# Differential heads moved beside the projections and the sliding heads, and the out-projection done whole, by token chunk, with the norm beside it

## The chip, the cores and the metric

The kernel runs on one core of a Trainium2 chip. Its time is the device time of one execution, in microseconds (us); the time of a kernel is the median of several executions. TensorE (PE) does the matmuls, VectorE (DVE), ScalarE (ACT) and GpSimd (POOL) the rest, and SyncE (SP) issues most of the DMAs.

## The reference, cut to what matters

Two layers of a trunk over 128 context tokens and 1024 latent tokens, 1024 wide. Each layer normalises its input, projects it to queries, keys and values of three groups of heads, attends, projects the heads' outputs and adds them to the residual; then a gated feed-forward part with a convolution over three positions.

```python
x_n = rmsnorm(x, g) * (1 + scale) + shift           # scale, shift, gate: from a modulation matmul
qa, ka, va, qb, kb, vb, qc, kc, vc = split(x_n @ w_in)   # A: 4 heads, B: 8 heads over 2 kv, C: 4 heads
oa = neighborhood_attn(qa, ka, va, cache, rpb)      # A: 8 rows x 16 columns around the token
ob = window_attn(qb, kb, vb, cache, sink)           # B: |i - j| <= 128, in blocks of 128
o1 = dense_attn(qc[0], kc[0], vc); o2 = dense_attn(qc[1], kc[1], vc)   # C: all 1024 + 256 keys
oc = rmsnorm(o1 - lam * o2, subln_g) * (1 - lam_init)
x = x + gate * (concat(oa, ob, oc) @ w_out)
x = x + gate2 * (silu(conv(h @ w_up)[g]) * conv(h @ w_up)[v]) @ w_down   # h: the norm of x again
```

## The kernel before

All of it is float32. A matrix that is to be multiplied is split into a high and a low part of a faster float32 form, and `gemm` (L488) makes three matmuls of each pair of blocks: high with high, high with low, low with high. `wload` (L366) loads a 128x1024 block of weights on SP's queue into `wraw` (two buffers), ACT writes the high part into `whl` (two buffers), and POOL or DVE subtracts for the low part. Activations lie transposed, with 128 features on the partitions and the 1156 token columns (128 context, 1024 latent, four of padding) in three chunks of some 386. So one block of 128 output features and one chunk of tokens over all 1024 input features is 24 matmuls.

A layer has 18 column blocks in its input projection (`inproj`), 54 groups of 24 gemms. Blocks 0 to 5 belong to the neighbourhood heads (A), 6 to 11 to the sliding heads (B), 12 to 17 to the differential heads (C). The queries and keys that it makes are normalised, turned by the rotary tables, split and written to DRAM, from where the attention loads them through POOL's queue.

The order of the work is that of the code, within what a scheduler that estimates times makes of it when the kernel is built: each engine gets one fixed row of instructions. `PLAN` names the steps of the input projection and of the heads that run in it: `A:4+2` projects blocks 4 and 2 side by side, `fA` opens the pool of the neighbourhood heads, `a:0` is head 0 of them, `b:0` the four sliding heads of one key and value head. In the order of the code a head stands ahead of the projections that come after it, so that these fill what it leaves free.

Every attention block is 128 queries. Its scores go to PSUM, in one of three banks named `s`; DVE takes the negative row maximum while it copies them into `P`; ACT takes the exponential with the row sum; PE transposes `P` in pieces of 128 into one of two banks `tb`; ACT copies these to `pt`; PE multiplies them with the values into the one bank `pv`; ACT copies the result into `O` (`tpv`, L644). Banks are given out in the order of the code. A differential head (`attnC`, L687) works on pairs of blocks, 256 queries, and has two components for each: scores, maxima and exponentials are made twice over 1280 keys, the second exponential is scaled and added to the first on POOL (L743, L744), and then one transpose and one product with the values do for both. The tiles `P` (128x1280) have seven buffers, and a head's queries and keys have two.

After the last step of `PLAN`, the four differential heads run in a pool of their own. Beside them stand the modulation pieces 4 to 11 (layer 0 only, four loads of 512 KB each) and, in `outproj_part`, the out-projection of the outputs of A (features 0 and 1) and B (2 to 5), whose raw outputs come back from the DRAM tile `odr`. This adds to the residual `x` in SBUF after each part. When the differential heads are done, the last part (features 6 and 7) follows, chunk 0 first and then chunks 1 and 2 together; `stats` squares the new `x` and `norm_apply` makes the feed-forward part's input of it. The last group of the down-projection goes the same way: chunk 0, then 1 and 2, and the norms of 1 and 2 behind both.

The change touches the main loop in `run`, `PLAN`, buffer numbers, `newO`, `finO`, the merge in `attnC`, and the weights `woa`, `wob`, `woc`.

## Time and profile before

| | |
|---|---|
| median of three runs | 3512.76 us (3512.06 to 3513.54) |
| the profiled execution | 3506.57 us |
| its span, first to last instruction | 3504.8 us |
| busy: PE, DVE, ACT, POOL | 95%, 58%, 43%, 35% |
| mean granted clock of TensorE | 0.971 |

The span falls into stages that repeat in both layers. Layer 0's first neighbourhood score starts at 147 us, the first sliding one at 313, the first differential one at 536; PE leaves attention at 889, ends the out-projection at 925 and runs the feed-forward part's gemms without a gap from 978 us on. In layer 1 these are 1907, 2075, 2301, 2597, 2637 and 2725. The feed-forward parts, some 770 us each, fill the rest.

PE's busy share is high everywhere and says little, because matmuls are pipelined and a matmul that has started late still counts as busy. What a stage leaves free is seen in the busy times of the other engines, in the granted clock, and in the number of matmuls that a stretch gets done. A group of instructions has its busy time (overlaps counted once), the mean of one in ns, and the idle time ahead of it.

### The profile page before, as it was taken

The page shows a single profiled execution, that of the slowest core. Times are in us where ns is not written, and L with a number is a line of the kernel's source. Part 1 is how long each engine was busy: PE and PEld are TensorE (multiplying, and loading weights), DVE is VectorE, ACT ScalarE, POOL GpSimd, SP SyncE. Part 2 cuts the span into 40 slices and gives each one's busy share as a digit, 9 for nine tenths or more (in the row PEclk, how much of TensorE's full clock was granted, in tenths as well). Part 3 has the DMA queues.
Part 4 walks back from the last instruction along what each step waited for, and adds up shares of the span by engine and source line. Part 5 has one row for each costly group of instructions (what it writes and reads, how often), then busy time and mean ns, then how long its engine had stood idle before and what let it go on. Part 6 is the DMA issues. An engine that isn't in the chain of part 4 may idle for free. (4 is left out here: it accounts for less than half of the span.)

```text
span 3504.8 us, 54130 instructions
## 1 busy us (share of the span) xinstructions
PE 3322.5 (95%) x20398; PEld 3012.4 (86%) x20398; DVE 2043.1 (58%) x4666; ACT 1505.4 (43%) x2905; POOL 1213.5 (35%) x1252
## 2 busy tenths in 40 slices
PE   6999998897899999999999989989888999999999
PEld 4987885684699999999989878858667999999999
DVE  5355466665676765676573554567667544544445
ACT  4566575545432222222245656665564322232222
POOL 6444246645611111111154442476565111111110
PEclk9999998897899999999999999999989999999999
DMA  5764338413112222222136652363201011111112
GB/s 202 203 162 130 94 100 217 133 37 93 34 61 73 85 76 67 82 85 78 43 125 189 169 134 74 109 165 82 52 17 36 32 46 44 43 37 46 46 40 93
DMA packets 184565, 318.21 MB, mean 91 GB/s; under 512 B 58544, under 2 KB 126528, under 8 KB 183920
## 3 DMA queue, kind: packets, MB, share of 16 engines
q1 hardware_dynamic: 170320, 266.18, 24.7%
q0 software_dynamic: 13984, 48.57, 6.8%
q8 instruction: 162, 2.65, 0.3%
q14 instruction: 99, 0.81, 0.1%
HBM read 260.15 MB, written 58.73 MB: 91 GB/s over the span
## 5 line engine op out<-in xcount | busy, mean ns | idle before, releaser
L496 PE MATMUL mm<-h,whl 128*128 128x386 f32 (+2 forms) x4488 | 888.0, 345 | 9.8 <-DVE h L484 4.3
L496 PEld LDWEIGHTS mm<-h,whl 128*128 128x128 f32 x4488 | 796.4, 190 | 29.3 <-DVE h L484 5.8
L496 PE MATMUL s<-h,whl 128*128 128x386 f32 (+2 forms) x4152 | 781.9, 342 | 15.7 <-ACT h L483 10.6
L496 PEld LDWEIGHTS s<-h,whl 128*128 128x128 f32 x4152 | 740.2, 190 | 29.9 <-ACT h L483 15.3
L378 POOL TENSOR_TENSOR whl<-wraw,whl 128x1024 fp32r<-128x1024 f32 x88 | 211.5, 2403 | 1344.5 <-ACT whl L377 1258.2
L685 ACT ACTIVATE P<-P,nm 128x641 f32<-128x641 f32 (+5 forms) x360 | 345.3, 960 | 169.5 <-DVE nm L734 89.6
L377 ACT ACTIVATE whl<-wraw 128x1024 fp32r<-128x1024 f32 (+1 forms) x210 | 207.5, 988 | 450.0 <-PE s L496 255.9
L496 PE MATMUL s<-ah,whl 128*128 128x384 f32 (+1 forms) x1268 | 356.6, 341 | 1.6 <-DVE x L918 1.2
L654 ACT ACTIVATE pt<-tb 128x512 f32<-128x512 f32 (+2 forms) x456 | 237.0, 541 | 147.2 <-PE tb L652 144.1
L652 PE MATMUL tb<-ident,P 128*128 128x128 f32 x1600 | 269.8, 289 | 14.9 <-ACT pt L654 7.5
L661 PE MATMUL pv<-pt,v 128*64 128x128 f32 x3200 | 264.0, 287 | 6.6 <-ACT pt L654 2.9
L918 DVE SCALAR_TENSOR_TENSOR x<-s,m,x 128x128 f32<-128x128 f32 (+3 forms) x347 | 170.0, 514 | 153.6 <-PE s L496 153.2
L918 DVE SCALAR_TENSOR_TENSOR x<-mm,m,x 128x128 f32<-128x128 f32 (+3 forms) x357 | 175.2, 513 | 142.1 <-PE mm L496 141.7
L652 PEld LDWEIGHTS tb<-ident,P 128*128 128x128 f32 x1600 | 189.7, 145 | 72.9 <-issue 36.3
L496 PE MATMUL mm<-ah,whl 128*128 128x384 f32 (+1 forms) x844 | 244.1, 340 | 1.4 <-DVE x L918 1.4
L661 PEld LDWEIGHTS pv<-pt,v 128*64 128x64 f32 x3200 | 173.7, 138 | 83.3 <-issue 54.6
L496 PEld LDWEIGHTS s<-ah,whl 128*128 128x128 f32 x1268 | 233.6, 189 | 5.9 <-DVE x L918 1.7
L496 PE MATMUL mm<-o,whl 128*128 128x384 f32 (+1 forms) x972 | 210.4, 354 | 11.7 <-ACT o L639 6.6
L496 PE MATMUL s<-al,whl 128*128 128x384 f32 (+1 forms) x634 | 215.1, 339 | 0.0
L496 PEld LDWEIGHTS mm<-o,whl 128*128 128x128 f32 x972 | 178.2, 197 | 24.5 <-issue 7.4
L682 PE MATMUL s<-k,q 128*128 128x256 f32 (+2 forms) x816 | 178.5, 333 | 19.2 <-DMA q<-d 11.5
L744 POOL TENSOR_TENSOR P<-P 128x1280 f32<-128x1280 f32 (+1 forms) x72 | 192.2, 2671 | 4.5
(208 smaller groups left out, 4971.8 us busy)
## 6 DMA issues: line engine op xcount, KB each, us to landing
wraw<-wup SPq DMA_DIRECT2D x88, 512.0 KB
mraw<-wmod SPq DMA_DIRECT2D x48, 512.0 KB
mraw<-wmv SPq DMA_DIRECT2D x96, 256.0 KB
wraw<-wdn SPq DMA_DIRECT2D x64, 384.0 KB
k<-d POOLq DMA_DIRECT2D x80, 288.5 KB, 6.5
wraw<-win SPq DMA_DIRECT2D x36, 512.0 KB
d<-hl SPq DMA_DIRECT2D x28, 386.0 KB
q<-d POOLq DMA_DIRECT2D x32, 289.0 KB, 6.6
```

The lines of the kernel that those rows point to most:

```text
L377: nc.scalar.activation(hl[:, 0, :n], raw[:, :n], AF.Copy)
L378: lo_eng.tensor_tensor(hl[:, 1, :n], raw[:, :n], hl[:, 0, :n].bitcast(F32), op=ALU.subtract)
L496: nc.tensor.matmul(ps, w_, r_[:, a:b], start=(i == 0), stop=(i == tot - 1))
L652: nc.tensor.transpose(t[:, 128 * j:128 * j + 128], it[0], self.ident)
L654: nc.scalar.activation(pt[:, :n], t[:, :n], AF.Copy)
L661: nc.tensor.matmul(ps[64 * i:64 * i + 64, :128], V[:, vb], pts[g // 4][:, 128 * (g % 4):128 * (g % 4) + 128], start=first[i], stop=left[i] ...
L682: nc.tensor.matmul(dst, q, view(ks[i]), start=(i == 0), stop=(i == 1))
L685: self.nc.scalar.activation(P[:, :n], P[:, :n], AF.Exp, scale=-1.0, bias=nm, accum_out=sums)
L744: nc.gpsimd.tensor_tensor(P2[0][:, :n], P2[0][:, :n], P2[1][:, :n], op=ALU.add)
L918: nc.vector.scalar_tensor_tensor(xx, ps[:, s - a:e - a], m[:, col + ob, v:v + 1], xx, op0=ALU.mult, op1=ALU.add)
```

## The change

- `PLAN` projects the C blocks beside the neighbourhood heads, then runs the differential heads 0 and 1 in front of the B blocks.
- After the projections, the differential heads 2 and 3 and all eight sliding heads run as two interleaved generators: after each step of a differential head (the context block, or a pair of blocks) four steps of the sliding heads (one block of queries each), and in layer 0 one modulation piece.
- The out-projection comes after all heads: for each token chunk, eight column blocks over all eight feature blocks, 24 gemms each, with the sums of squares behind each column block and the chunk's norm behind the eighth. Its weights are loaded once for each chunk, 24 loads of 512 KB a layer where there were 8; the low part is made by DVE and POOL in turn. The outputs of A and B are read back from `odr` in `loado`, and split as before.
- In `attnC` the merge of the two components goes to DVE for the first block of a pair and the context block, in one operation, and stays on POOL for the second.
- The last group of the down-projection goes chunk by chunk, each with its norm, and loads its weights three times and not twice.
- `P` of the differential heads has five buffers for seven, the projections' `t` six for seven; queries, keys and values of the sliding heads have more. Pools change sides from layer to layer.

```diff
-PLAN = "A:4+2 A:0 A:5+3 A:1 mF fA a:0 a:1 a:2 a:3 xA B:11 B:10+6 B:7+8 fB b:0 B:9 b:1 xB C:16 C:17 C:14+12 C:15+13"
+PLAN = "A:4+2 A:0 A:5+3 A:1 mF fA a:0 a:1 a:2 a:3 xA C:16 C:14+12 C:17 C:15+13 fC c:0 c:1 B:11 B:10+6 B:7+8 B:9"
-NQ_B, NK_B, NV_B, NP_B, NT_B = 3, 2, 1, 6, 5
-NQ_C, NK_C, NV_C, NP_C, NT_C = 2, 2, 1, 7, 4
+NQ_B, NK_B, NV_B, NP_B, NT_B = 4, 4, 2, 6, 6
+NQ_C, NK_C, NV_C, NP_C, NT_C = 2, 2, 1, 5, 4
...
-                cp, cs = self.open("C")
-                self.attnC(cp)
+                bp, bps = self.open("B")
+                gb = self.chain(self.attnB(bp, kv) for kv in range(2))
+                for n, _ in enumerate(self.chain(self.attnC(ap, h) for h in (2, 3))):
+                    for _ in range(4):
+                        next(gb, None)
+                    if todo and n > 0:
+                        self.mod_piece(l, todo.pop(0), md, self.mm(), NMC)
+                for _ in gb:
+                    pass
...
-                self.outproj_part(x, ab, 0, 2, a["woa"][l])
...
-                self.outproj_part(x, ab, 2, 4, a["wob"][l])
...
-                for ts in ((0,), (1, 2)):
+                for t in range(3):
+                    c0, c1 = OCHUNK[t]
                     for ob in range(KT):
-                        if ob % 4 == 0:
-                            whl = self.wload(a["woc"][l, ob // 4], nc.vector)
...
+                        whl = self.wload(a["wo"][l, ob], nc.gpsimd if ob % 2 else nc.vector)
+                        ps = self.mm()
+                        self.gemm(ps[:, :c1 - c0], whl, range(8), None, ow[t], 0, c1 - c0)
+                        self.addx(x, ob, ps, c0, c1, 16)
+                        self.stats(np_, x, stats[t], t, [ob])
+                    self.norm_apply(np_, hp0 if t == 0 else hp1, x, stats[t], t, "f")
...
-                for ts in ((0,), (1, 2)):
+                for t in range(3):
...
-                    self.down(x, *last, ts, after)
+                    self.down(x, *last, (t,), after)
...
+    def loado(self, pool, t):
...
+            nc.sync.dma_start(hl.bitcast(F32), self.odr[k, :, c0:c1])
+            nc.scalar.activation(hh, hl.bitcast(F32), AF.Copy)
+            nc.gpsimd.tensor_tensor(hl, hl.bitcast(F32), hh.bitcast(F32), op=ALU.subtract)
...
-                    nc.vector.scalar_tensor_tensor(ss[:, 1:2], ss[:, 1:2], lam[:, 1:2], ss[:, 0:1], op0=ALU.mult, op1=ALU.mult)
-                    nc.gpsimd.tensor_scalar(P2[1][:, :n], P2[1][:, :n], ss[:, 1:2], 0.0, op0=ALU.mult, op1=ALU.add)
-                    nc.gpsimd.tensor_tensor(P2[0][:, :n], P2[0][:, :n], P2[1][:, :n], op=ALU.add)
+                    nc.vector.tensor_scalar(ss[:, 1:2], ss[:, 1:2], ss[:, 0:1], lam[:, 1:2], op0=ALU.mult, op1=ALU.mult)
+                    if i == 0:
+                        nc.vector.scalar_tensor_tensor(P2[0][:, :n], P2[1][:, :n], ss[:, 1:2], P2[0][:, :n], op0=ALU.mult, op1=ALU.add)
+                    else:
+                        nc.gpsimd.tensor_scalar(P2[1][:, :n], P2[1][:, :n], ss[:, 1:2], 0.0, op0=ALU.mult, op1=ALU.add)
+                        nc.gpsimd.tensor_tensor(P2[0][:, :n], P2[0][:, :n], P2[1][:, :n], op=ALU.add)
```

How the change moves instructions is seen in the built programs' rows. In them `h` is a split chunk of the normalised input, `o` and `oc` are split outputs of the heads, `whl` weights, `mraw` modulation weights, `k`, `q`, `v`, `P` and `pt` the tiles of attention; `mm`, `s`, `tb` and `pv` are PSUM banks. Line numbers of the changed kernel differ a little: the same line stands four lower up to L728 (L496 is now L492), and L768 is L769.

The first place is PE in a differential head of layer 1. Before, its scores (L732) stand among small groups of output gemms:

```order
L661 MATMUL pv<-pt,v 64x128 x4
L673 MATMUL tb<-ident,sums 128x128 x4
L732 MATMUL s<-k,q 128x512
L496 MATMUL mm<-o,whl 128x386 x6
L661 MATMUL pv<-pt,v 64x128 x4
L652 MATMUL tb<-ident,P 128x128
L496 MATMUL mm<-o,whl 128x384
L732 MATMUL s<-k,q 128x512
L496 MATMUL mm<-o,whl 128x384 x3
L732 MATMUL s<-k,q 128x512
```

Now the scores of head 0 (L728) stand among groups of projection gemms:

```order
L728 MATMUL s<-k,q 128x512 x2
L728 MATMUL s<-k,q 128x256 x2
L492 MATMUL mm<-h,whl 128x386 x22
L728 MATMUL s<-k,q 128x512
L492 MATMUL mm<-h,whl 128x386
L728 MATMUL s<-k,q 128x512
L492 MATMUL mm<-h,whl 128x386
L728 MATMUL s<-k,q 128x512
L519 MATMUL mm<-t,ones_88 128x386
L583 MATMUL mm<-ident,qg 128x128 x3
L492 MATMUL mm<-h,whl 128x384 x21
```

The filler moved from the output gemms, which end in one DVE addition for each 6 or 12 of them, to the projection's, which end in a norm and a rotation for each 24. From head 0's first score to the first sliding score stand 456 of them in layer 1.

The second place is PE in layer 0 around the modulation pieces (L392, now L388). Before, they stand between the differential heads' scores:

```order
L732 MATMUL s<-k,q 128x256
L392 MATMUL mm<-mraw,cvz 32x512 x2
L732 MATMUL s<-k,q 128x256
L661 MATMUL pv<-pt,v 64x128 x4
L652 MATMUL tb<-ident,P 128x128
L732 MATMUL s<-k,q 128x512
L392 MATMUL mm<-mraw,cvz 32x512 x2
L732 MATMUL s<-k,q 128x512
L396 MATMUL mm<-sel,mrow 128x2 x4
```

Now this stands between the end of head 1 and the first sliding score (L678); two L388 matmuls use one load:

```order
L388 MATMUL mm<-mraw,cvz 32x512 x6
L769 MATMUL tb<-sq,ones_86 128x386
L648 MATMUL tb<-ident,P 128x128
L657 MATMUL pv<-pt,v 64x128
L388 MATMUL mm<-mraw,cvz 32x512 x2
L392 MATMUL mm<-sel,mrow 128x2 x4
L519 MATMUL mm<-t,ones_86 128x386
L388 MATMUL mm<-mraw,cvz 32x512 x8
L392 MATMUL mm<-sel,mrow 128x2 x4
L388 MATMUL mm<-mraw,cvz 32x512 x8
L392 MATMUL mm<-sel,mrow 128x2 x4
L388 MATMUL mm<-mraw,cvz 32x512 x6
```

So 30 of the 64 modulation matmuls, and with them 15 loads, stand ahead of the first sliding score, where before they were spread over the heads.

The third place is POOL in layer 0's norm for the feed-forward part, at chunk 1 of the out-projection. Now the low parts of weights (L374) stand between the steps of the norm (L475) and the sums of squares (L452):

```order
L374 TENSOR_TENSOR whl<-wraw,whl 128x1024
L452 TENSOR_TENSOR nsq<-nsq 128x386
L475 TENSOR_SCALAR nh<-nh,gf_8609,m_104 128x128
L475 TENSOR_SCALAR nh<-nh,gf_8609,m_104 128x256
L475 TENSOR_SCALAR nh<-nh,gf_8609,m_104 128x128
L475 TENSOR_SCALAR nh<-nh,gf_8609,m_104 128x256
L475 TENSOR_SCALAR nh<-nh,gf_8609,m_104 128x128
L475 TENSOR_SCALAR nh<-nh,gf_8609,m_104 128x256
L452 TENSOR_TENSOR nsq<-nsq 128x386
L475 TENSOR_SCALAR nh<-nh,gf_8609,m_104 128x128
L475 TENSOR_SCALAR nh<-nh,gf_8609,m_104 128x256
L374 TENSOR_TENSOR whl<-wraw,whl 128x1024
```

Before, POOL made no low part for the out-projection (DVE made all eight); the norm's steps ended with those of chunks 1 and 2 in one row, and the feed-forward part's weights followed:

```order
L479 TENSOR_SCALAR nh<-nh,gf_9293,m_107 128x128
L479 TENSOR_SCALAR nh<-nh,gf_9293,m_107 128x256
L444 TENSOR_TENSOR ny<-ny 128x386
L444 TENSOR_TENSOR ny<-ny 128x388
L479 TENSOR_SCALAR nh<-nh,gf_9293,m_107 128x386 x16
L378 TENSOR_TENSOR whl<-wraw,whl 128x1024 x42
```

What moved is that twelve low parts a layer now wait in POOL's row among the norm's steps.

## Rows read from the trace of the kernel before

**Rows 1.** Busy us of each engine (records), granted clock, DMA share, GB/s, by stage.

```profile
147.00:313.00 166.00, 158.15 (x1104) 136.53 (x1103) 85.39 (x239) 103.87 (x243) 74.84 (x102) 0.99 0.58 150
313.00:536.00 223.00, 218.61 (x1743) 191.01 (x1743) 123.20 (x393) 145.04 (x340) 87.72 (x162) 0.99 0.41 106
536.00:889.00 353.00, 303.79 (x1941) 214.90 (x1939) 210.73 (x628) 183.62 (x339) 200.68 (x163) 0.88 0.41 115
925.00:978.00 53.00, 43.64 (x201) 37.20 (x200) 45.72 (x67) 26.09 (x47) 38.63 (x34) 0.94 0.09 30
1907.00:2075.00 168.00, 156.25 (x1106) 135.57 (x1104) 86.62 (x241) 104.16 (x243) 76.05 (x105) 0.98 0.59 150
2075.00:2301.00 226.00, 223.01 (x1741) 192.33 (x1741) 124.77 (x395) 146.03 (x343) 88.29 (x168) 0.98 0.43 106
2301.00:2597.00 296.00, 256.46 (x1747) 200.09 (x1745) 200.98 (x611) 173.77 (x323) 193.15 (x151) 0.93 0.29 76
2637.00:2725.00 88.00, 78.35 (x382) 69.35 (x381) 70.32 (x118) 35.54 (x60) 41.02 (x36) 0.94 0.09 31
```

**Rows 2.** The same view, PE, PEld, DVE, ACT, POOL, for short stretches.

```profile
675.00:700.00 25.00, 18.52 (x96) 8.85 (x93) 9.88 (x33) 10.33 (x19) 17.97 (x22) 0.89 0.97 245
2215.00:2290.00 75.00, 75.00 (x593) 63.60 (x592) 47.48 (x143) 54.01 (x126) 36.93 (x68) 1.00 0.37 99
2310.00:2340.00 30.00, 26.84 (x202) 17.05 (x200) 24.70 (x91) 24.83 (x46) 23.08 (x15) 1.00 0.61 210
2365.00:2415.00 50.00, 49.04 (x345) 41.51 (x345) 40.22 (x126) 30.56 (x54) 34.64 (x25) 0.98 0.18 53
2526.00:2595.00 69.00, 54.71 (x367) 36.72 (x367) 42.71 (x133) 41.13 (x74) 44.91 (x25) 0.83 0.10 20
```

**Rows 3.** Timeline of PE in the feed-forward part: start, us, instructions.

```profile
2700.30 4.41 PE L496 MATMUL mm<-h,whl 128*128 128x386 f32 x24
2704.55 4.40 PE L496 MATMUL s<-h,whl 128*128 128x388 f32 x24
```

**Rows 4.** DVE groups: differential stage (two), sliding stage (two), L770 (ns min/median/max).

```profile
L734 DVE CUSTOM_DVE_ANT_0 P<-s,zero,nm 128x512 f32<-128x512 f32 (+1 forms) x128 | 76.0, 611 | 17.8 <-PE s L732 16.1
L740 DVE RECIPROCAL sums<-ss 128x1 f32<-128x1 f32 x32 | 5.1, 159 | 7.8 <-ACT P L685 7.6
...
L538 DVE TENSOR_TENSOR qg<-qg,rope 128x386 f32<-128x386 f32 (+1 forms) x15 | 10.6, 707 | 0.2
L443 DVE SCALAR_TENSOR_TENSOR t<-mm,t 128x386 f32<-128x386 f32 (+1 forms) x15 | 8.4, 557 | 11.2 <-ACT t L442 11.2
...
L770 DVE SCALAR_TENSOR_TENSOR O<-O,pp,oy x12: 604/682/3239, 692.3 to 2603.0; 128x386 f32<-128x386 f32 x8, 128x384 f32<-128x384 f32 x4
```

**Rows 5.** The larger of POOL's two merge operations, differential stage of layer 1.

```profile
L744 POOL TENSOR_TENSOR P<-P 128x1280 f32<-128x1280 f32 (+1 forms) x36 | 95.4, 2653 | 2.3
```

**Rows 6.** ACT groups: sliding stage of layer 1 (three), differential stage (two).

```profile
L685 ACT ACTIVATE P<-P,nm 128x641 f32<-128x641 f32 (+2 forms) x68 | 51.4, 758 | 33.6 <-DVE nm L821 16.4 <-issue 13.9 <-DVE nm L815 2.2
L665 ACT ACTIVATE O<-pv 128x128 f32<-128x128 f32 x32 | 8.8, 276 | 20.3 <-PE pv L661 20.2
L589 ACT ACTIVATE qg<-mm 128x384 f32<-128x384 f32 x6 | 2.9, 478 | 0.5 <-PE mm L587 0.4
...
L685 ACT ACTIVATE P<-P,nm 128x1280 f32<-128x1280 f32 (+3 forms) x76 | 93.1, 1226 | 38.2 <-DVE nm L734 37.7 <-DVE sums L740 0.4
L665 ACT ACTIVATE O<-pv 64x128 f32<-64x128 f32 (+1 forms) x40 | 10.8, 271 | 27.9 <-PE pv L661 27.4
```

**Rows 7.** POOL groups from 2597 to 2725, out-projection's end and norm of layer 1.

```profile
L479 POOL TENSOR_SCALAR nh<-nh,gf,m 128x386 f32<-128x386 f32 (+2 forms) x32 | 29.7, 938 | 4.6 <-ACT h L483 2.9 <-DVE nh L477 1.7
L456 POOL TENSOR_TENSOR nsq<-nsq 128x386 f32<-128x386 f32 (+1 forms) x12 | 15.1, 1269 | 5.5 <-ACT nsq L452 5.4
L378 POOL TENSOR_TENSOR whl<-wraw,whl 128x1024 fp32r<-128x1024 f32 x6 | 14.4, 2406 | 43.0 <-ACT whl L377 42.9
L640 POOL TENSOR_TENSOR o<-O,o 128x384 fp32r<-128x384 f32 (+1 forms) x6 | 5.6, 966 | 0.0
```

151 lines of the change are left out of this document (67 added, 84 removed).

## The prediction

> **What bounds the kernel now.** The first view is the table of busy time by stage, cut at the first scores of each kind of head [rows 1]. In both layers the stage of the neighbourhood heads (166 and 168 us) and that of the sliding heads (223 and 226 us) have projection gemms between their own matmuls, and PE is busy for 93% or more. The stage of the differential heads is the loose one: 353 us in layer 0 and 296 us in layer 1, with PE at 86 and 87%, DVE at 60 and 68%, ACT at 52 and 59%, POOL at 57 and 65%, and a granted clock of 0.88 and 0.93. No engine is full there. The short stretches say why [rows 2]: at 2310 to 2340, with no gemm beside, DVE and ACT reach 82 and 83% of the time; at 2365 to 2415, with output gemms beside, DVE reaches 80%; at 675 to 700, where layer 0 waits for modulation weights, DVE and ACT fall to 40% while the queues move 245 GB/s. Then come 36 and 40 us for the last part of the out-projection (889 to 925 and 2597 to 2637) and the norm's tail: 201 PE records in 53 us, 382 in 88 us [rows 1]. A gemm takes 4.25 us for 24 when nothing stops it, 0.177 us [rows 3], so 53 - 201 x 0.177 = 17 us and 88 - 382 x 0.177 = 20 us are lost there. The region that the change rewrites is thus 166 + 223 + 353 + 36 + 17 = 795 us in layer 0 and 168 + 226 + 296 + 40 + 20 = 750 us in layer 1.
>
> **The change, part by part.** *Stage 1, the neighbourhood heads*, keeps its order and about its number of gemms; the fill comes from the C columns now. I leave it at 166 and 168 us.
>
> *Stage 2, heads 0 and 1 beside the B columns.* It holds two differential heads and 456 gemms, and DVE is the first limit. Seven DVE rows of the four heads, from 76.0 us to 5.1 us, sum to 174, so 87 for two [rows 4]. The projections cost DVE 3.0 us a q or k chunk (five rows, from 0.707 us down to 0.557), and 16 chunks make 48. New on DVE is the merge of the second component for every other block, one operation over 128x1280 with two SBUF inputs, eight in the stage. No row has it. The nearest is L770 over 386 columns: 0.604 us at best, 0.682 in the median, 3.239 at worst [rows 4]. Scaled by columns the best is 2.0 us; the worst adds the same delay once, 4.6 us. I take 2.3, by the median, and have 18 us. The sum is 153 us of durations. Durations overlap: in the old sliding stage twelve ACT rows, from 51.4 us to 2.9, sum to 169 us [rows 6] where ACT was busy for 146 [rows 1], a factor of 0.87. That gives 133 us busy; at 80% it is 166 us, at the old stage's 68% it is 196. I take 195, the upper end, because six weight splits are not in the sum and because 72 of the 456 gemms are still to come when the second head's scores end, and the sliding heads' keys can be loaded only behind the last of them. POOL gives up half of its merges, whose larger half alone took 95.4 us for four heads [rows 5]; it was no limit, so that is worth nothing by itself.
>
> *Stage 3, heads 2 and 3 with all sliding heads.* No gemm is left as filler but layer 0's modulation pieces, and ACT is the first limit. Four ACT rows of the sliding heads, from 51.4 us to 8.8, sum to 116 us for 32 of 36 query blocks, so 130; four of the differential heads, from 93.1 us to 10.8, sum to 169, half is 84 [rows 6]. These 214 us of durations are 186 us busy. At the 83% of the best stretch that is 225 us, at the 72% of 2215 to 2290 [rows 2] it is 258, at the old differential stage's 59% it is 317. I take 255: two streams without gemms in PE's queue should do a little better than 72%, but the first loads and the last head's tail are in it too. PE is not the limit: in layer 1's old sliding stage 223 us of PE less 456 x 0.177 leave 142 us for 1285 attention records, 0.111 us each at most, and 2103 records (36/32 of these and half of the differential stage's 1315) make 233 us at most. In layer 0 fifteen modulation loads stand ahead of the first sliding score in PE's order, as its rows above show: 7.9 MB at 245 GB/s [rows 2] are 32 us, of which the loads of keys would take some 10 anyway. So layer 0 gets 275 us; before, its pieces lay in three places and cost 353 - 296 = 57.
>
> *Stage 4, the out-projection.* 576 gemms at 0.177 us are 102 us. Most of them ran beside heads before; now they stand alone, and beside them run the norm, 24 splits of outputs and 24 weight loads in place of 8. POOL has 29.7 + 15.1 us of norm, 12 weight splits at 2.406 us and 24 output splits at 0.966 us [rows 7]: 97 us, nearly as much as PE. PE runs 24 gemms, 4.25 us, between one weight and the next, and POOL's order, shown above, has eight norm operations and a sum of squares between two weights. I give 12 us for weights that come late, 8 for the entry from attention, 3 for sums of squares and 3 for the exit (the last norm has 96 gemms, 17 us, of other chunks to hide behind): 128 us. Bounds: 113 if POOL is never late, 150 if each of 12 weights waits for three norm operations of 0.938 us [rows 7]. This replaces the 36 + 17 and 40 + 20 us, and it is where the gain goes that stages 2 and 3 make.
>
> *The last down-projection* by chunk has 12 weight loads for 8 and a norm beside it; DVE was 80% busy in a norm's tail already (70.32 of 88 us [rows 1]), so I give it 4 us of gain, between 0 and 8. Pools, sides and smaller buffers are priced at nothing: five P buffers for seven make a pair's second block wait for the first one's merge, which the other stream covers in stages 2 and 3; uncovered, the wait is an exponential (1.226 us [rows 6]) and the merge, 3.5 us a pair and 28 us for the eight pairs of a stage.
>
> **The sum.** Layer 0: 166 + 195 + 275 + 128 = 764, 31 less. Layer 1: 168 + 195 + 255 + 128 = 746, 4 less. With 4 for the passage between layers it is 39 us. The profiled execution took 3506.6 us around its span of 3504.8, so 3468; the median of the runs is 6.2 us above it, hence **3474 us**.
>
> **A rule against it.** L770 shows what a DVE operation on SBUF may take: 3.239 us where 0.604 do [rows 4]; POOL's merges beside it take 2.653 us each [rows 5]. The Trainium skill (SBUF — State Buffer, "SBUF: two separate sides") says that a DVE operation with two SBUF inputs and a GpSimd operation hold one port pair by an exclusive lock, and that the loser waits for the whole instruction. By that, each merge on DVE could cost 2.3 us more than I gave it; in stage 2, where DVE sets the pace, sixteen in both layers make 37 us, and the total would be 3511 us; the trace agrees in the worst case, not in the median.
>
> **Rivals.** (a) *The two streams fill each other*: ACT at 83% and DVE at 80%, stages of 225 and 166 us, 59 less a layer, **3356 us**. For it: the stretch without a gemm. Against it: that lasted 30 us. Chance 0.20. (b) *The two streams wait for each other's banks*, the slower side: three banks for scores, two for transposes and one for PV are given out in program order, so a late sliding block holds up a differential one behind it. With ACT at 63% stage 3 takes 295 us, 40 more a layer, **3554 us**. It decides from about 275 us on, where the total equals that of before. For it: with seven P buffers, heads alone had ACT at 60% at 2526 to 2595 [rows 2]. Chance 0.20. (c) *POOL holds up the weights*: stage 4 at 150 us, **3518 us**. For it: 97 us of POOL beside 105 of PE; against it: the old norm's tail lost only 20. Chance 0.13. (d) *The clock falls without gemms*, as to 0.83 at 2526 to 2595 [rows 2]: 233 us at that clock are 281, 26 more a layer, **3526 us**; against it the clock of 1.00 at 2310 to 2340 with no gemm either. Chance 0.05. The Trainium skill (TensorE: Matmul & The Clock Gate, "Part 4: PE-mode transpose") says that full clock does not engage for transposes; the trace does not agree where scores and PV stand between them. (e) The forecast, 3430 to 3505 us: 0.42.
>
> **Chances.** 0.2% is 7 us, about what a measurement of this kernel can tell from no change. Faster: (a), 0.40 of the forecast, 0.03 of (c): 0.63. Same: 0.02 of the forecast, 0.05 of (c): 0.07. Slower: (b), (d), 0.05 of (c): 0.30. The range leaves out half of (a) and half of (b): 3360 to 3555 us.
>
> **What would show it.** Cut the new profile at the first score of each kind of head: stage 2 at 166 to 196 us with DVE at 68 to 80%; stage 3 at 225 to 295 us with ACT first, longer in layer 0 with a low clock at its start; stage 4 at 113 to 150 us with POOL about as busy as PE. The forecast is wrong if ACT in stage 3 is outside 65 to 80%, if the DVE merge has a mean outside 2.0 to 4.6 us, or if weights and not gemms set stage 4.

## The result, and the profile after

The changed kernel takes 3649.75 us (3647.89 to 3650.73) where the kernel before takes 3512.41 in the same session: a ratio of 1.0392, 95% interval 1.0374 to 1.0410. That is 137 us slower, where 39 us faster were forecast. In the experiments below the kernel before ran in each session; its medians lie between 3506 and 3512 us, so ratios are compared, and 0.1% is 3.5 us.

The page of the changed kernel begins so (busy us, then the clock in tenths over 40 slices of 91 us):

```profile
span 3648.0 us, 54000 instructions
PE 3370.6 (92%) x20398; PEld 3042.0 (83%) x20398; DVE 2070.1 (57%) x4590; ACT 1537.8 (42%) x2941; POOL 1148.6 (31%) x1196
PEclk9998997998999999999999999879989999999999
```

The busy sums differ little from before (PE has 48 us more, POOL 65 less). The stages do differ. This is the table by stage, as [rows 1] has it for before: us from and to, the length, busy us of each engine with its records, granted clock, DMA share, GB/s. The cuts are the first score of the neighbourhood heads, of head 0, of the sliding heads, the end of attention on PE, and the last output matmul; layer 0, then layer 1.

```profile
155.20:330.60 175.40, 163.32 (x1137) 142.95 (x1135) 79.94 (x227) 102.44 (x239) 66.89 (x89) 0.97 0.53 133
330.60:591.60 261.00, 205.95 (x1172) 154.56 (x1172) 163.07 (x403) 130.02 (x248) 147.88 (x164) 0.84 0.50 135
591.60:888.00 296.40, 266.26 (x2061) 185.35 (x2059) 165.79 (x577) 187.46 (x413) 65.88 (x120) 0.92 0.29 82
888.00:1010.00 122.00, 112.80 (x587) 108.07 (x588) 65.37 (x83) 53.68 (x90) 92.85 (x73) 0.94 0.35 114
1974.70:2144.60 169.90, 159.38 (x1096) 137.40 (x1094) 73.68 (x219) 98.91 (x235) 63.11 (x85) 0.96 0.55 140
2144.60:2401.50 256.90, 186.45 (x1114) 152.61 (x1115) 172.53 (x408) 131.57 (x252) 153.72 (x166) 0.85 0.41 104
2401.50:2676.00 274.50, 241.68 (x1945) 174.86 (x1945) 159.61 (x570) 184.04 (x407) 65.54 (x123) 0.92 0.23 59
2676.00:2799.50 123.50, 113.50 (x592) 107.36 (x592) 67.31 (x83) 54.12 (x90) 94.18 (x74) 0.95 0.36 119
```

| us | before, layers 0, 1 | forecast | after |
|---|---|---|---|
| stage 1, neighbourhood heads | 166, 168 | 166, 168 | 175, 170 |
| stage 2, heads 0 and 1 (before: sliding heads) | 223, 226 | 195, 195 | 261, 257 |
| stage 3, the other heads | 353, 296 | 275, 255 | 296, 275 |
| stage 4, out-projection and norm | 53, 60 | 128, 128 | 124, 126 |

Stage 4 runs to the start of the feed-forward part, taken as the time when 144 of its matmuls are done less 144 x 0.177 us (1037.4 - 25.5 = 1011.9 and 2827.1 - 25.5 = 2801.6). The column for before has the numbers that the prediction counted. By the same rule for the start of the feed-forward part (944.7 and 2657.8 before), the layers became 58 and 76 us longer, and layer 0 starts its heads 9 us later: the 143 us by which the span grew. The stage that stands out is the second, with PE busy for only 79 and 73% and a clock of 0.84. Cut in three, layer 1's shows why: up to head 1's end, up to the last projection matmul, and up to the first sliding score.

```profile
2144.60:2327.00 182.40, 157.04 (x959) 129.66 (x960) 140.72 (x355) 109.17 (x203) 108.61 (x106) 0.92 0.36 94
2327.00:2364.50 37.50, 26.34 (x149) 21.91 (x150) 21.53 (x37) 16.29 (x36) 23.15 (x21) 0.82 0.45 118
2364.50:2401.50 37.00, 3.06 (x9) 1.03 (x8) 10.28 (x17) 6.11 (x14) 21.97 (x40) 0.55 0.60 138
```

Layer 0, cut in two where head 1 ends, looks the same:

```profile
330.60:515.00 184.40, 158.33 (x958) 129.57 (x959) 139.26 (x354) 109.70 (x204) 106.21 (x105) 0.90 0.35 94
515.00:591.60 76.60, 47.62 (x216) 24.99 (x214) 23.81 (x49) 20.32 (x44) 41.68 (x60) 0.70 0.86 232
```

Its second part also holds the modulation matmuls (L388) that stand ahead of the first sliding score, and PE waits 17.7 us for their loads.

In layer 1's last 37 us PE is busy for 3. PE's row and POOL's row in that stretch (start, us, engine, line, operation, what ended the idle time before) show the way from the last projection matmuls to the first sliding score:

```profile
2369.76 1.66 PE L519 MATMUL mm<-t,ones 128*128 128x386 f32 x2 [1.62 <-ACT qg L517]
2401.51 0.66 PE L678 MATMUL s<-k,q 128*128 128x128 f32 x2 [30.09 <-DMA q<-d]
...
2383.57 1.00 POOL L559 TENSOR_TENSOR hl<-qg,hl 128x386 fp32r<-128x386 f32 x1 [1.23 <-ACT hl L558]
2387.60 2.11 POOL L614 DMA_DIRECT2D k<-d  x4 [3.04 <-DMA d<-hl]
2389.69 2.08 POOL L604 DMA_DIRECT2D q<-d  x4
```

The last column's norm, rotation and split go on until 2384.6; behind the split, in POOL's row, stand the loads of the sliding heads' keys and queries, which wait for the column's store (d<-hl). The last load of these rows is issued by 2391.8, and the first score runs 10 us later. I call these 37 us the drain.

### The profile page after: what moved, and what is told of

It reads as the page before. It is cut to its first block, busy times and chain, and to the rows that moved or that the text cites. A ratio compares the mean times of both kernels' runs of the same rounds, so it can differ in the third digit from the quotient of the medians.

```text
span 3648.0 us, 54000 instructions
## 1 busy us (share of the span) xinstructions
PE 3370.6 (92%) x20398; PEld 3042.0 (83%) x20398; DVE 2070.1 (57%) x4590; ACT 1537.8 (42%) x2941; POOL 1148.6 (31%) x1196
## 5 line engine op out<-in xcount | busy, mean ns | idle before, releaser
L492 PE MATMUL mm<-h,whl 128*128 128x386 f32 (+2 forms) x4488 | 884.9, 347 | 15.2 <-DVE t L439 12.5
L492 PEld LDWEIGHTS mm<-h,whl 128*128 128x128 f32 x4488 | 808.6, 193 | 35.1 <-DVE t L439 19.7
L492 PE MATMUL s<-h,whl 128*128 128x386 f32 (+2 forms) x4152 | 769.5, 341 | 7.4 <-ACT h L479 5.7
L492 PEld LDWEIGHTS s<-h,whl 128*128 128x128 f32 x4152 | 740.1, 190 | 12.8 <-ACT h L479 6.9
L374 POOL TENSOR_TENSOR whl<-wraw,whl 128x1024 fp32r<-128x1024 f32 x112 | 270.1, 2412 | 1364.5 <-ACT whl L373 1276.5
L373 ACT ACTIVATE whl<-wraw 128x1024 fp32r<-128x1024 f32 (+1 forms) x246 | 243.9, 992 | 530.2 <-PE s L492 284.4
L681 ACT ACTIVATE P<-P,nm 128x1280 f32<-128x1280 f32 (+5 forms) x360 | 345.0, 960 | 156.9 <-DVE nm L730 70.5
L492 PE MATMUL s<-ah,whl 128*128 128x384 f32 (+1 forms) x1270 | 356.5, 342 | 4.2 <-DVE whl L374 2.2
L648 PE MATMUL tb<-ident,P 128*128 128x128 f32 x1600 | 283.8, 297 | 43.4 <-POOL P L743 23.2
L492 PE MATMUL mm<-ah,whl 128*128 128x384 f32 (+1 forms) x842 | 243.0, 341 | 1.5 <-DVE x L921 1.2
L678 PE MATMUL s<-k,q 128*128 128x256 f32 (+2 forms) x816 | 195.3, 348 | 51.0 <-DMA q<-d 32.1
L492 PEld LDWEIGHTS s<-ah,whl 128*128 128x128 f32 x1270 | 234.1, 189 | 9.3 <-DVE whl L374 2.9
L492 PE MATMUL s<-al,whl 128*128 128x384 f32 (+1 forms) x635 | 215.3, 339 | 0.0
L678 PEld LDWEIGHTS s<-k,q 128*128 128x128 f32 x816 | 130.7, 198 | 92.4 <-issue 52.5
L728 PE MATMUL s<-k,q 128*128 128x512 f32 (+2 forms) x400 | 151.3, 433 | 60.7 <-DMA k<-d 32.2
L374 DVE TENSOR_TENSOR whl<-wraw,whl 128x768 fp32r<-128x768 f32 (+1 forms) x134 | 157.4, 1175 | 61.0 <-ACT whl L373 57.4
L966 ACT ACTIVATE ah<-yv 128x384 fp32r<-128x384 f32 x132 | 69.4, 526 | 278.8 <-DVE yv L964 278.8
```

The lines of the kernel that those rows point to most:

```text
L373: nc.scalar.activation(hl[:, 0, :n], raw[:, :n], AF.Copy)
L374: lo_eng.tensor_tensor(hl[:, 1, :n], raw[:, :n], hl[:, 0, :n].bitcast(F32), op=ALU.subtract)
L492: nc.tensor.matmul(ps, w_, r_[:, a:b], start=(i == 0), stop=(i == tot - 1))
L648: nc.tensor.transpose(t[:, 128 * j:128 * j + 128], it[0], self.ident)
L678: nc.tensor.matmul(dst, q, view(ks[i]), start=(i == 0), stop=(i == 1))
L681: self.nc.scalar.activation(P[:, :n], P[:, :n], AF.Exp, scale=-1.0, bias=nm, accum_out=sums)
```

## Experiments on what the moved heads cost

My first theory was an order on PE: head 2's context score runs at 2327, but its pairs stand behind the first sliding blocks in PE's row, and so behind the drain. The rival: the drain's own work holds the engines that head 2 wants.

**Sliding blocks only behind head 2** (e1).

```diff
-                    for _ in range(4):
+                    for _ in range(7 if n > 3 else 0):
                         next(gb, None)
```

> The changed kernel, but the sliding heads' blocks begin only behind the last pair of differential head 2 (seven at a time instead of four). Theory: the 75 us between head 1's end and the first sliding score in layer 1 (2327 to 2401, PE 29 us busy) are lost because the first sliding blocks stand in PE's row ahead of head 2's pairs, and so behind the drain of the B columns. Then head 2's four pairs fill that stretch, the stretch from there to the end of attention gets 40 to 55 us shorter a layer, and the time is 3540 to 3570 us. Rival: DVE and POOL are held by the drain itself (norms, rotations, splits of the last columns), so head 2 crawls there and nothing is gained: 3630 us or more.

3646.57 us, ratio 1.0382 (1.0365 to 1.0399), the changed kernel's within the intervals. Layer 1 in three stretches: heads 0 and 1, head 2, then head 3 and nearly all sliding blocks.

```profile
2142.60:2330.00 187.40, 157.74 (x933) 130.57 (x933) 144.83 (x355) 108.30 (x203) 105.26 (x101) 0.90 0.31 87
2330.00:2425.30 95.30, 65.34 (x362) 46.59 (x362) 69.46 (x174) 50.27 (x95) 62.08 (x77) 0.78 0.53 120
2425.30:2653.00 227.70, 202.51 (x1717) 148.02 (x1715) 118.31 (x448) 152.51 (x354) 46.56 (x109) 0.94 0.18 39
```

Head 2 did fill the drain, but took 95 us in it, with 72 projection matmuls (13 us) beside. DVE is busy for 73% of them. From head 0's first score to the last product with the values, layer 1's attention took 521 us for 526. These 5 us went again at the next seam: the sliding heads now end last, and the out-projection waits for their outputs' way through DRAM (waits of PE from 2640 to 2690: us in total, times, longest):

```profile
PE mm L492 <- ACT o L285: 18.0, 2, 12.5
```

**Head 2 in the plan, ahead of the B columns** (e2; three heads beside them, eight blocks a step beside head 3):

```diff
-... fC c:0 c:1 B:11 B:10+6 B:7+8 B:9"
+... fC c:0 c:1 c:2 B:11 B:10+6 B:7+8 B:9"
```

> The changed kernel, but differential head 2 stands ahead of the B columns too, so three heads run beside them and only head 3 beside the sliding heads (eight blocks a step). By the theory of the drain the columns end before head 2 does and the keys of the sliding heads arrive beside it: stage 2 stays at 250 to 265 us with three heads in it for two, stage 3 falls to 190 to 215 us, and the time is 3540 to 3580 us. By the rival that DVE sets the pace of stage 2, three heads make it 300 us or more, and the time is 3630 us or more.

3646.57 us, ratio 1.0384 (1.0369 to 1.0399). The first sliding score came at 2433.7, 289 us behind head 0's first, with three heads in them. That is near the rival's number (300 us or more), and far from the theory's (250 to 265).

**No interleave** (e6).

```diff
-                    for _ in range(4):
-                        next(gb, None)
```

> The changed kernel without the interleave: differential heads 2 and 3 first, then all sliding heads alone. In the kernel with the out-projection alone a differential head without matmuls beside it takes some 57 us, and 36 sliding blocks with 456 projection matmuls (81 us) take 222 us, so 3.9 us a block without them. If the two streams take turns instead of filling each other (additive: 114 + 141 = 255 us, as the changed kernel measured), undoing the interleave costs nothing or brings something, since head 2 also stands in the drain: 3610 to 3660 us. If the interleave does fill gaps, its loss costs 30 us or more a layer: 3700 us or more.

3650.58 us, ratio 1.041 (1.039 to 1.043): the interleave brings nothing that can be measured. The sliding heads alone, layer 1 (the last 27 of their 36 blocks):

```profile
2543.50:2647.80 104.30, 104.27 (x1006) 82.52 (x1004) 57.71 (x226) 79.72 (x207) 12.06 (x68) 1.00 0.13 36
```

That is 3.86 us a block, with PE busy the whole time at full clock. Before, 36 blocks with 456 projection matmuls beside them took 226 us; less 81 us for these matmuls (0.177 us each) that is 4.0 us a block. So the time of a sliding block and that of the matmuls beside it add up. Sliding blocks do not leave PE free for a differential head; they fill its row by themselves.

**Columns in another order** (e5), so that sliding blocks are ready at the drain, and **the value column last** (e9), so that the drain is a short one:

```diff
-... C:16 C:14+12 C:17 C:15+13 fC c:0 c:1 B:11 B:10+6 B:7+8 B:9"
+... C:16 C:14+12 B:11 B:10+6 fC c:0 c:1 C:17 C:15+13 B:7+8 B:9"
...
+                for _ in range(6):
+                    next(gb, None)
                 for n, _ in enumerate(self.chain(self.attnC(ap, h) for h in (2, 3))):
```

> The changed kernel with its columns in another order: the keys, values and first queries of the sliding heads (11, 10, 6) beside the neighbourhood heads, and C:17 C:15+13 B:7+8 B:9 behind the differential heads 0 and 1; six sliding blocks stand ahead of head 2. So neither the first sliding blocks nor the last differential ones wait for the last columns' norm, rotation, store and load. Theory of the drain: the 75 us from head 1's last scores to the first sliding scores were 13 us of matmuls and some 60 of drain, and filling them with head 2 moved the drain's DVE and POOL work into head 2; with the drain behind sliding blocks that are ready, 25 to 50 us a layer come back: 3550 to 3600 us. Rival, that heads and projections cost their sum in any order and the loss lies elsewhere: 3630 us or more.

```diff
-... fC c:0 c:1 B:11 B:10+6 B:7+8 B:9"
+... fC c:0 c:1 B:10+6 B:7+8 B:9 B:11"
```

> The changed kernel with one word of the plan moved: the sliding heads' value column (11) last among the projections, not first of theirs. Its drain is a copy, a transpose and a store; the last query column's norm, rotation, split and store (37 us from the last matmul to the first sliding score) then run beside its 72 matmuls. If the drain of the last query column stands open in the changed kernel, 12 to 20 us a layer come back: 3610 to 3625 us. If heads and projections cost their sum whatever stands last, 3640 us or more.

The first gave 3640.07 us, 1.0388 (1.0366 to 1.0411); the second 3651.44, 1.0414 (1.0397 to 1.0432). Neither brought anything clear. In the first the sliding heads' keys had long been stored, and the first sliding score still came at 2402.6: their loads stood in POOL's row behind the last column's split, as in the rows above. In the second, the stretch from the last projection matmul to the first sliding score did halve, but the matmuls ended later by nearly as much (234 us behind head 0's first score, where it was 220):

```profile
2145.70:2380.00 234.30, 191.81 (x1109) 155.33 (x1109) 176.81 (x408) 128.90 (x246) 143.24 (x136) 0.88 0.34 95
2380.00:2398.50 18.50, 1.30 (x8) 0.66 (x7) 0.00 (x0) 2.34 (x5) 11.80 (x31) 0.58 1.05 211
```

So the order on PE, my first theory, falls. The second theory is that the projection's norms and rotations are DVE and POOL work, as the differential heads' maxima and merges are. Beside these heads the columns fall behind, and what is late stands open behind head 1. Before, the columns stood beside the neighbourhood and sliding heads, where DVE is busy for half of the time ([rows 1]). This is tested by taking the same work out of both kernels.

**The rotation left out of both**, and with it the loads of the rotary tables: of the changed kernel (e13) and of the kernel before (e14).

```diff
-                if g != "A":
+                if False:
                     if (g, ci) not in self.rope:
```

> The changed kernel with the rotation of the sliding and differential columns left out (three DVE operations of 0.56 to 0.7 us and one of POOL of some 1.1 us for each of 27 chunks a layer, no matmul), so its queries and keys are not rotated. In the changed kernel 15 of the 27 stand beside the differential heads 0 and 1. Theory of the pairing: DVE and POOL pace stage 2, since the heads that want most of them (differential) now stand beside the columns that want them too; 15 chunks of 2.9 us come off that chain: 15 to 40 us a layer, 3570 to 3620 us. If PE's row or the drain's transfers pace it, 0 to 8 us a layer: 3635 to 3650 us.

> The kernel before with the same rotation left out, the other half of the pair. There the 27 chunks stand beside the neighbourhood and the sliding heads, where DVE is busy for 55% and PE for 98%. By the theory of the pairing the rotation is covered there: 3490 to 3507 us. If its gain is that of the changed kernel, the place of the columns has nothing to do with the loss.

The changed kernel fell to 3578.9 us, 1.0194 (1.0179 to 1.021). That is about 69 us, or 2.0% of the time before, less than with the rotation (1.0392). The kernel before gave 3504.03, 0.9981 (0.9969 to 0.9993), 7 us less. Layer 1 by stage, the changed kernel first (stages 1 to 3), then the kernel before (neighbourhood, sliding, differential heads):

```profile
1944.50:2123.70 179.20, 173.57 (x1205) 152.92 (x1204) 66.99 (x197) 110.00 (x256) 66.72 (x87) 0.99 0.55 139
2123.70:2318.70 195.00, 163.01 (x937) 129.51 (x938) 116.01 (x310) 113.40 (x213) 121.22 (x138) 0.88 0.48 116
2318.70:2608.00 289.30, 253.63 (x2014) 182.63 (x2015) 167.39 (x582) 191.49 (x424) 65.69 (x120) 0.91 0.17 46
```

```profile
1894.90:2080.30 185.40, 179.80 (x1243) 158.94 (x1242) 70.28 (x201) 114.30 (x263) 72.04 (x103) 1.00 0.53 141
2080.30:2289.70 209.40, 198.50 (x1614) 169.38 (x1614) 97.50 (x331) 138.41 (x334) 67.52 (x150) 0.99 0.36 92
2289.70:2583.00 293.30, 257.27 (x1740) 200.24 (x1738) 206.94 (x606) 171.93 (x315) 190.29 (x145) 0.91 0.28 72
```

Stage 2 of the changed kernel is 195 us instead of 257, stages 1 and 3 are 9 and 15 longer. Its last projection matmul is at 2251.8, ahead of head 1's last score at 2305.5, where it was 45 us behind it; the stretch without matmuls is gone. In the kernel before the same three stages hold 688 us where they held 690. Two things limit the reading. The rows are laid out anew when the kernel is built, and without the rotation 489 and not 393 projection matmuls stand in layer 1's stage 1 (528 and not 408 in the kernel before). And the edit takes the rotation out of all 27 chunks of a layer, of which 12 (the C columns) stand beside the neighbourhood heads in the changed kernel too. So the runs show that leaving out the rotation is worth 69 us in the one arrangement and 7 in the other, and that stage 2 is the place of it; they do not show how much of it is engine time and how much is the layout.

**Which engine.** Two of POOL's steps of the sliding columns on DVE (e17), and one more buffer `t` (e18):

```diff
-QY = {"A": "p", "B": "p", "C": "p"}
+QY = {"A": "p", "B": "v", "C": "p"}
...
-                    nc.gpsimd.tensor_tensor(sw, sw, cs[:, 1], op=ALU.mult)
+                    (nc.vector if g == "B" else nc.gpsimd).tensor_tensor(sw, sw, cs[:, 1], op=ALU.mult)
```

> The changed kernel with two of POOL's steps for the sliding columns moved to DVE: the rotation's product with the sine table and the product with the reciprocal root (some 1.0 and 1.1 us on POOL, about 0.6 each on DVE, 15 chunks a layer). Taking out the whole rotation brought 71 us where the kernel before lost only 7. If DVE's load paces stage 2, 15 x 1.2 us more of it cost 8 to 18 us a layer: 3665 to 3690 us. If POOL's part, the way from DVE to POOL and back behind its merges, paces it, the columns come through sooner: 3600 to 3635 us.

```diff
-NT_I, NQG_I, NHL_I, NR_I = 6, 5, 2, 2
+NT_I, NQG_I, NHL_I, NR_I = 7, 5, 2, 2
```

> The changed kernel with seven buffers for the projection's t, as before, in place of six (a chunk takes four of them, so six hold one and a half chunks). If what paces the columns in stage 2 is that a chunk waits for the buffers of the chunk before it, one more brings 5 to 20 us a layer: 3610 to 3640 us. If the engines' load paces it, nothing: 3643 to 3655 us.

3641.74 us, 1.0371 (1.0354 to 1.0389), and 3642.3, 1.0381 (1.0366 to 1.0397), with intervals that overlap the changed kernel's. Steps moved from POOL to DVE brought nothing, and neither did the `t` buffer; that POOL's relief was used up by DVE's load is not excluded.

The trace does show one thing that the two engines do to each other. These are the rotation's last addition, with two SBUF inputs, in layer 1's stage 2 and beside the sliding heads before (busy us, mean ns of one | idle before), and then one of them in DVE's row, and POOL's row at that time:

```profile
L535 DVE TENSOR_TENSOR qg<-qg,t 128x386 f32<-128x386 f32 x12 | 14.2, 1182 | 3.4 <-POOL t L533 3.2
L539 DVE TENSOR_TENSOR qg<-qg,t 128x386 f32<-128x386 f32 x10 | 5.6, 563 | 2.6 <-POOL t L537 2.3
...
2288.40 3.23 DVE L535 TENSOR_TENSOR qg<-qg,t 128x386 f32<-128x386 f32 x1 [0.16 <-POOL t L533]
...
2288.33 2.90 POOL L743 TENSOR_TENSOR P<-P 128x1280 f32<-128x1280 f32 x1
```

The addition took 3.23 us, where the median is 0.56. POOL's merge had started 0.07 us ahead of it, and the addition ended 0.4 us behind the merge. So DVE waits inside its instruction for POOL, which counts as busy time. But this does not set the length of the stage. With all merges on DVE (e16, below) the same group and layer 1's stage 2 are:

```profile
L535 DVE TENSOR_TENSOR qg<-qg,t 128x386 f32<-128x386 f32 x12 | 6.7, 556 | 3.9 <-POOL t L533 3.8
2128.60:2384.70 256.10, 188.29 (x1114) 152.76 (x1114) 169.58 (x416) 130.91 (x252) 116.64 (x150) 0.86 0.40 104
```

The additions no longer wait, and the stage is 256 us long as it was. What holds the columns stays open.

## Experiments on the out-projection

**The out-projection part alone** (e3), in the kernel before: heads in their old places, merges on POOL, seven `P` buffers, the out-projection and the last down-projection by chunk as in the change.

```diff
-                cp, cs = self.open("C")
-                self.attnC(cp)
...
-                self.outproj_part(x, ab, 0, 2, a["woa"][l])
...
-                self.outproj_part(x, ab, 2, 4, a["wob"][l])
...
+                for n, _ in enumerate(self.chain(self.attnC(cp, h) for h in range(4))):
+                    if todo and n % 2 == 0:
+                        self.mod_piece(l, todo.pop(0), md, self.mm(), NMC)
...
+                for t in range(3):
...
+                        self.gemm(ps[:, :c1 - c0], whl, range(8), None, ow[t], 0, c1 - c0)
```

> The kernel before with the out-projection part of the change alone (all of it behind the heads by token chunk, the norm beside it, and the last down-projection by chunk); heads in their old places, merges on POOL, seven P buffers. If stage 4 costs here what it does in the changed kernel (142 to 146 us from the end of attention where 56 to 61 were), and the four heads without output gemms get faster by 25 to 35 us a layer only, the time is 3600 to 3640 us, and this part is the larger share of the loss. If the heads get faster by the whole 68 us that 384 gemms take, it is 3535 to 3550 us.

3579.94 us, 1.0197 (1.018 to 1.0214): half of the changed kernel's loss. In layer 1 the time from head 0's first score to head 3's last fell from 277 us (2300.9 to 2577.9) to 227 (2335.7 to 2562.5), and from there to the feed-forward part it rose from 80 (2657.8) to 164.5 (2727.0). In layer 0 these are 330 to 261 and 80 to 154. 432 output matmuls, 76 us (the expectation counts 384), had cost layer 1's heads 50 us and layer 0's 68; behind the heads they cost 85 and 74. That makes 35 us in layer 1 and 5 in layer 0, 40 of the 69. The rest lies in layer 1's sliding heads, 245 us for 226, and in a start that is 10 us later. Here too the rows were laid out anew: layer 1's sliding heads have 504 projection matmuls beside them where there were 456. So these 29 us are not shown to come from the out-projection's place.

**Low parts of the output weights all on DVE** (e4), in the changed kernel:

```diff
-                        whl = self.wload(a["wo"][l, ob], nc.gpsimd if ob % 2 else nc.vector)
+                        whl = self.wload(a["wo"][l, ob], nc.vector)
```

> The changed kernel with all low parts of the out-projection's weights made by DVE, none by POOL. If POOL's row holds up the weights (the rival that the prediction named), stage 4 gets 10 to 20 us a layer shorter: 3610 to 3630 us. If it is the entry from attention and PE's own 110 us that set it, the gain is 0 to 5 us a layer: 3640 to 3650 us.

3643.45 us, 1.0373 (1.0358 to 1.0389): some 3 us a layer, and the intervals overlap the changed kernel's. The 10 to 20 us a layer that were expected of POOL holding up the weights are not there.

**The norm beside the next chunk alone** (e12), for features 6 and 7 of the kernel before with half of its merges on DVE (the base is e8 in the next section):

```diff
-                for ts in ((0,), (1, 2)):
+                for t in range(3):
...
-                    if ts == (0,):
-                        self.norm_apply(np_, hp0, x, stats[0], 0, "f")
+                    self.norm_apply(np_, hp0 if t == 0 else hp1, x, stats[t], t, "f")
```

> The kernel before with the merge of the first block of a pair on DVE (3495 us) and, in the last part of the out-projection (features 6 and 7) alone, the change's idea of chunk by chunk: each chunk with its norm behind its eighth column block, the weights loaded three times and not twice. If a norm beside the next chunk's 48 matmuls (8.5 us) hides some of the 54 us that are lost between the last head and the feed-forward part, it brings 5 to 12 us a layer: 3470 to 3485 us. If 8.5 us are too little cover and the weights come late, 3492 to 3505 us.

3492.43 us, 0.9963 (0.9948 to 0.9978), against 0.9964 without: it brings nothing.

## Experiments on the merge and the buffers

**All merges on POOL** in the changed kernel (e7), then **all on DVE** (e16):

```diff
-                    if i == 0:
+                    if False:
                         nc.vector.scalar_tensor_tensor(P2[0][:, :n], P2[1][:, :n], ss[:, 1:2], P2[0][:, :n], op0=ALU.mult, op1=ALU.add)
```

> The changed kernel with all merges back on POOL, as before, still five P buffers. A merge on DVE has a median of 1.55 us where one on POOL takes 1.34 + 2.93 us, and POOL's is waited for by transposes. If DVE's share of stage 2 (77%) is what sets it, taking 16 merges off DVE there brings 10 to 25 us: 3625 to 3640 us. If the merge's length sets when a pair's transposes can start, it costs 10 to 50 us: 3660 to 3700 us.

```diff
-                    if i == 0:
+                    if True:
```

> The changed kernel with all merges on DVE. If the length of a merge is what a pair waits for, with five P buffers above all, the second half brings what the first half brought (43 us): 3600 to 3625 us. If DVE paces stage 2 by its busy time, eight more merges of 1.55 us a layer there take some of it back: 3635 to 3660 us.

3693.55 us, 1.0534 (1.0512 to 1.0555), and 3625.1, 1.0332 (1.0315 to 1.035). So each half of the merges that goes to DVE makes the changed kernel faster, by about 50 and 21 us (the ratios' differences, 1.42 and 0.60%). The groups of the changed kernel (busy us, mean ns of one | idle before):

```profile
L740 DVE SCALAR_TENSOR_TENSOR P<-P,ss 128x1280 f32<-128x1280 f32 x32 | 52.2, 1631 | 0.5
L743 POOL TENSOR_TENSOR P<-P 128x1280 f32<-128x1280 f32 x32 | 96.8, 3025 | 1.5
L742 POOL TENSOR_SCALAR P<-P,ss 128x1280 f32<-128x1280 f32 x32 | 44.5, 1390 | 100.4 <-DVE ss L738 61.7 <-ACT oc L635 30.9 <-ACT t L437 2.6
```

A merge is one step of 1.63 us on DVE and two of 4.4 us together on POOL. Two things could make the shorter one pay: PE's transposes wait for the merge (23.2 us in all for POOL's merges in the changed kernel), and DVE's additions wait for POOL's merges, as shown above. The runs do not part the two.

**The same in the kernel before**: half of the merges on DVE as in the change (e8), then all (e11).

```diff
+                    if i == 0:
+                        nc.vector.scalar_tensor_tensor(P2[0][:, :n], P2[1][:, :n], ss[:, 1:2], P2[0][:, :n], op0=ALU.mult, op1=ALU.add)
+                    else:
                         nc.gpsimd.tensor_scalar(P2[1][:, :n], P2[1][:, :n], ss[:, 1:2], 0.0, op0=ALU.mult, op1=ALU.add)
```

> The kernel before with this one part of the change: the merge of the first block of a pair and of the context block on DVE. If the merge's length sets when transposes start, the 330 us of the two differential stages that are head boundaries and pairs get 10 to 40 us shorter: 3470 to 3500 us. If output matmuls fill whatever the merge leaves, or the DVE and POOL operations hold each other up, 3505 to 3530 us.

> The kernel before with all merges of the differential heads on DVE. If the length of the merge (1.55 us on DVE, 1.34 + 2.93 us on POOL) sets when a pair's transposes can start, as moving half of them brought 13 us, the other half brings as much again: 3475 to 3488 us. If DVE, busy for 68% of that stage, becomes the limit, 3495 to 3510 us.

3494.74 us, 0.9964 (0.9953 to 0.9975), and 3482.82, 0.993 (0.9915 to 0.9945). The second beats both kernels, by 0.7% and 4.4%. DVE was not the limit, though it is busy for 78% of the differential stage (first line below, layer 1). The second line is the group of its merges in both layers:

```profile
2273.20:2575.00 301.80, 265.59 (x1750) 200.27 (x1748) 236.51 (x650) 176.92 (x326) 57.18 (x81) 0.91 0.28 74
L744 DVE SCALAR_TENSOR_TENSOR P<-P,ss 128x1280 f32<-128x1280 f32 x64 | 105.3, 1645 | 0.3
```

**Five P buffers** in the kernel before with half of the merges on DVE (e10), and **eight** in the one with all of them there (e15):

```diff
-NQ_C, NK_C, NV_C, NP_C, NT_C = 2, 2, 1, 7, 4
+NQ_C, NK_C, NV_C, NP_C, NT_C = 2, 2, 1, 5, 4
```

> The kernel before with the merge of the first block of a pair on DVE (3495 us) and five P buffers for seven. The prediction priced the smaller buffers at nothing where another stream stands beside, and at 28 us for eight pairs where none does. Output matmuls stand beside about half of the pairs here: 3495 to 3505 us if they cover it; 3530 us or more if a pair waits for the merge in any case.

```diff
-NM0, NMC = 8, 3
+NM0, NMC = 8, 2
-NQ_C, NK_C, NV_C, NP_C, NT_C = 2, 2, 1, 7, 4
+NQ_C, NK_C, NV_C, NP_C, NT_C = 2, 2, 1, 8, 4
```

> The kernel before with all merges on DVE (3483 us) and eight P buffers for seven (paid with one buffer of modulation weights, which only layer 0 uses). Seven to five cost 50 us: if the stall goes on to shrink with more buffers, 5 to 15 us less, 3468 to 3478 us; if seven are enough for two pairs and the spare buffer was needed in layer 0, 3480 to 3495 us.

Five: 3544.75 us, 1.0108 (1.0093 to 1.0123), 1.44% or 50 us more than its base. Layer 1 bears most of it: from head 0's first score to head 3's last 316 us (2305.3 to 2621.6) instead of 264 (2295.5 to 2559.5). The loads of head 0 are issued 16 us ahead of its first score in both, so it is not their place in POOL's row. Eight: 3547.26 us, 1.0104 (1.0088 to 1.0119), 61 us more than its base, which neither theory expected. In layer 1, which has no modulation pieces, the loads of head 0's queries and keys are issued at 2314.2, behind the split of the last column:

```profile
2313.27 1.02 POOL L563 TENSOR_TENSOR hl<-qg,hl 128x386 fp32r<-128x386 f32 x1 [0.23 <-ACT hl L562]
2314.22 2.01 POOL L699 DMA_DIRECT2D q<-d  x4
```

With seven buffers they stand ahead of the last chunks' steps:

```profile
2257.47 2.01 POOL L699 DMA_DIRECT2D q<-d  x4
...
2275.05 1.00 POOL L563 TENSOR_TENSOR hl<-qg,hl 128x386 fp32r<-128x386 f32 x1 [1.06 <-ACT hl L562]
```

So with the larger pool the loads stand behind the drain, as in the changed kernel. That the pool lies over the projection's tiles, which are free only then, is my explanation; it was not tried apart. In layer 0 the buffer of modulation weights that paid for it costs too: PE waits 29.5 us for such weights at the start of its differential heads, and the heads end 35 us later (875.5 for 840.3). The two costs are not separated. Seven `P` buffers in the changed kernel were not run.

## Why the prediction was wrong

**Stage 2 is the step that failed**: forecast 195 us, with 166 and 196 as its ends, measured 261 and 257. Of the 176 us between the forecast of 3474 and the result, the two stages 2 hold 128, the stages 3 41 and the stages 1 11; the stages 4 came out 6 us shorter. Two terms of stage 2 were mis-sized.

The first is DVE's work: 133 us busy were worked out, and it was busy for 163 and 173. In layer 1 the five rows of the columns took 66 us in place of 48 (19 chunks passed and not 16, and some additions waited for POOL), and seven weight splits that were not in the sum took 15. The part up to the end of head 1 took 184 and 182 us, with DVE at 76 and 77%, where 166 were reckoned.

The second, and the larger, is the rest: for the matmuls that are still to come when head 1 ends, 72 in layer 1, and for the loads behind them, I had 29 us, by taking the upper end of a range that came from busy shares. They took 77 and 75 us. In layer 0 the modulation matmuls lie there too. The prediction had put its 20 us for their loads into stage 3, though by its own cut they stand ahead of the first sliding score, and so in stage 2.

The prediction had costed the columns as DVE time to be added to the heads' (48 us) and had not followed a column's chain, through ACT, DVE and POOL in turn, beside heads that want DVE and POOL. e13 and e14 point there: leaving out the rotation is worth 69 us in the changed kernel and 7 in the kernel before, new layouts included. Which link of the chain holds the columns is not shown, since neither the moved steps (e17) nor the buffer (e18) nor the end of the waits for POOL (e16) made stage 2 clearly shorter.

**The out-projection is the other large loss**, 69 us by itself (e3), and no single term of mine was wrong there: stage 4 was forecast at 128 us and took 124 and 126, with POOL at 93 and 94 us busy. But the gain that was to pay for it did not come in the heads: their stages 2 and 3 together were forecast at 470 and 450 us and took 557 and 531. e3 shows what the output matmuls cost in their old place: 118 us in two layers, for 153 us of matmuls. Moving them out of the heads freed less than they take alone, and the norm beside the next chunk brought nothing where it was tried, for features 6 and 7 (e12). That the 69 us of e3 and the 69 us of e13 come to the 137 us of the loss is not shown to be more than chance: they were measured in different kernels, both with new layouts, and the merges and the `P` buffers, worth some 50 us each, lie beside them. The move of the heads without the out-projection was not run.

**Stage 3** was forecast at 275 and 255 us and took 296 and 275, within its range of 225 to 295 but for one us, with ACT at 63 and 67% where 65 to 80 were named. For layer 0 the 275 held the 20 us of modulation loads; PE waited for such loads only 2.0 us there, so the heads alone were 41 us over. The size was nearer than in stage 2, the picture behind it was not right. Two streams were to do "a little better than 72%"; e6 shows that they do no better together than one behind the other. And PE was not free: a lone sliding block takes 3.86 us with PE busy throughout, where the prediction had set PE aside with 233 us "at most" for the stage; it was busy for 242 of 275.

**The merge** was priced as a load, 18 us a layer on DVE, and POOL's relief as worth nothing. A merge takes 1.63 us and not 2.3, below the 2.0 that were named as its lower end, and with all merges on POOL the changed kernel is 50 us slower (e7). **Buffers** were priced at nothing, which was wrong too: five P for seven cost 50 us in the old arrangement (e10). The prediction gave 28 us a stage as the price without cover and then took the cover for granted. How much of it is in the changed kernel is open.

**The rule against it** came from the Trainium skill (SBUF — State Buffer, "SBUF: two separate sides"): a two-input DVE operation and a GpSimd operation exclude each other for a whole instruction. The trace agrees: at 2288 the rotation's addition waited out a merge on POOL, 3.23 us for 0.56. But the prediction put the price on the wrong operations. The DVE merges of 128x1280 took 2.42 us at worst; what waited more were the columns' additions, for the merges that had stayed on POOL, and taking more merges off POOL helped each time.

**Rivals.** (a) fell: ACT at 63 to 67%. (b) gave the right sign, but stage 3 was 275 us and not 295 in layer 1, and its 3554 us were still 96 too low. (c) fell with stages 4 of 124 and 126 us, and with e4. (d) fell for stage 3 (clock 0.92); the clock was lower in stage 2, 0.84 and 0.85, where PE was busy for only 79 and 73%. No rival but the rule above made stage 2 longer, and its range was closed at 196 us.
